# A decoder layer on one core: the first projection without its norm, x on a second queue, and another request order at the MLP's third pair

## The chip, the cores and the metric

The kernel runs on one core of one Trainium2 chip. The metric is the device time of one execution in microseconds, as the median of several runs. The engines are TensorE (PE), VectorE (DVE), ScalarE (ACT), GpSimd (POOL) and SyncE (SP). DMAs are issued by the queues of SP, ACT and POOL.

## What is computed

The reference is one layer of a decoder on 2048 tokens of width 1024, in fp32: a norm, a combined input projection, three causal mixers, an output projection, a gated MLP with a short convolution, and a gated embedding.

```python
h = rmsnorm(x, norm_mix_gain[i])
z = h @ w_in[i]
...
y = jnp.concatenate([y_a, y_b, y_c], axis=-1).astype(dt)
x = x + y @ w_out[i]
x = x + conv_ffn(rmsnorm(x, norm_ffn_gain[i]), ffn_w_up[i], ffn_conv_w[i], ffn_w_down[i])
gate = jax.nn.sigmoid((x @ ple_w_gate[i]).astype(jnp.float32))
x = x + (gate * (p[i] @ ple_w_proj[i]).astype(jnp.float32)).astype(dt)
return rmsnorm(x, final_norm_gain)
```

`rmsnorm(x, g)` is x times 1/sqrt(mean(x^2) + eps) times g. The factor 1/sqrt(...) is one number for each token, so it can also be multiplied into the result of `h @ w_in`.

## The kernel before

**Tiling.** Tokens lie along the free dimension, width along the 128 partitions. There are two halves of 1024 tokens (the loop over `hf`, L465), and each half has two chunks of 512 (`cks`). A tile of 128x1024 (`t4`, from one pool of 40) is one eighth of the width for one half, or two eighths for one chunk.

**fp32 products.** Every operand is split into a high part (ACT copies it, rounded) and a low part (DVE subtracts), by `split` (L256). `mm3` (L264) then makes three matmuls: high x high, high x low and low x high (L265, L266, L267). A tile `h` holds high and low of one eighth of one chunk side by side.

**Weights.** They come as a stream in a fixed order (`wlist`, L210 to L227). `w_get` (L243) hands out a unit and runs the stream ahead by a number of units (`ahead`). A raw unit of 512 KB is loaded on SP's queue into one of three `wr` buffers, then split into `wh` and `wl` (for the projections), or into `wt` tiles (for the MLP, where sums `s` of weight quarters are split too).

**The start (L448 to L461).** SP loads the first chunk of x as four pairs of eighths (`xl`), then constants, the first weight, the vector of gains, the second weight and the second chunk. `Norm.add` squares each eighth on ACT and adds on DVE. `rstd` sums over the partitions by small matmuls into `pm` and takes 1/sqrt in a chain of small DVE steps with one on ACT. `bcast` spreads the result over the partitions by matmuls into `pr`. `h_apply` (L416) multiplies x by the gain and by `pr` (DVE, into `hx`) and splits into `h`.

**The input projection** has 24 units (`IN_UNITS`), each one tile of 128 output rows: two chunks x eight k x three = 48 matmuls into a PSUM pair `pz` (a pool of two). `gemm` (L566) runs the first two units jointly: chunk 0 of both, then chunk 1 of both, so that chunk 1's `h` is wanted later. `evac` (L559) hands a finished PSUM pair to the mixers' functions (`hg_f`, `hg_q`, ..., L557). The mixers' chains (`hg_chain` and two others) run between the projection's steps: `weave` (L593) and `fill` (L584) draw a number of steps of `gemm` between steps of a chain. At the start of the first half `fill` runs eleven steps before and between the second chunk's norm (L728 to L731).

**The MLP** has 22 pairs of gate and up tiles; three matmuls of quarters are saved by sums of weights and of h (the tiles X[0] to X[7]). `up_first` (L879) makes the pairs 0 and 1 together. Its last products go into `pbc`, and after those of pair 0 it does pair 0's convolutions, silu, product and split, and the last steps of `h2`, which makes X[7] and X[4]. `up(j)` (L934) makes the pairs from 2 on; its first product, `pa`, is here called the third pair's start. After every second pair `down_pair` (L965) multiplies two pairs' results with the down weights into `pdn`; ACT copies that to `st`, and POOL's queue adds it to DRAM. `stats_steps` (L1007) loads the next half's x by eighths and squares it for the next norm, one step after each `up(j)`.

**What sets the order.** The instructions are put into each engine's queue by a scheduler, which may put an instruction ahead of others that the program names first; each engine then works its queue in order. Waits between engines follow the data, and the buffers of the pools.

Of the kernel before, what the change touches and what calls it, by code (L numbers as in the profile page):

```python
# [20 lines left out]
CH = 512  # L21
# [27 lines left out]
def trunk(ctx, tc, xT, pT, w_in, w_out, w_up, w_down, w_pp, w_pg, wr_bd, wi_bd, vecs, consts, masks, out):  # L49
# [40 lines left out]
    def cks(c):  # L90
        return slice(c * CH, (c + 1) * CH)
# [187 lines left out]
    def run(g):  # L279
        for _ in g:  # L280
            pass
# [141 lines left out]

    def stats_stream(hf, c):
        n = Norm()
        for k in range(KD):
            s = t2("xs")
            nc.gpsimd.dma_start(s, xT[k, :, hf * TH + c * CH : hf * TH + (c + 1) * CH])
            n.add(s)
        n.rstd()  # L430
        return n
# [16 lines left out]
    x_load(x0[0], 0, 0, nc.sync)  # L448
    nc.sync.dma_start(kt, consts[:, :KBLK])
    w_upto(1)  # L450
    nc.sync.dma_start(vt, vecs)
    w_upto(2)
    x_load(x0[1], 0, 1, nc.sync)
    norms = [Norm(), Norm()]
    for k in range(KD):
        norms[0].add(x0[0][k])
    norms[0].rstd()
    pr = norms[0].bcast()
    for k in range(KD):
        norms[1].add(x0[1][k], nc.gpsimd, True)  # L460
    run(h_apply(h[0], x0[0], "g1", pr))  # L461
# [3 lines left out]
    for hf in range(NH):  # L465
# [93 lines left out]
        def evac(m, ps):  # L559
            for b0, fn in EVAC:  # L560
                if b0 <= m < b0 + (3 if b0 < 18 else 2):
                    fn(m - b0, ps)
# [3 lines left out]
        def gemm():  # L566

            ws, pss = [w_get("in", hf, m) for m in IN_UNITS[:2]], [ps2("pz"), ps2("pz")]
            for c in range(NC):
                for i in range(2):  # L570
                    yield from proj_gen(pss[i][:, cks(c)], ws[i], h[c])
                    if c == NC - 1:
                        evac(IN_UNITS[i], pss[i])
                        done[0] += 1
            for m in IN_UNITS[2:]:
                w, ps = w_get("in", hf, m), ps2("pz")
                for c in range(NC):
                    yield from proj_gen(ps[:, cks(c)], w, h[c])
                evac(m, ps)
                done[0] += 1  # L580
# [146 lines left out]
        if first:  # L727
            fill(6)  # L728
            norms[1].rstd()
            fill(5)  # L730
            run(h_apply(h[1], x0[1], "g1", norms[1].bcast(), (1, 3, 5)))  # L731
            with tc.issue_after(last_split[0].ins), tc.issue_after(last_split[1].ins):
                derived()
            t = t4("blk")[:, :P]
            nc.scalar.dma_start(t, consts[:, KBLK:])
            ACT(blk, t, AF.Copy)
# [141 lines left out]

        def up_first():  # L879
# [33 lines left out]
            for j in pairs:  # L913
                for i in range(2):
                    prod(sums1[j][i], w[j, 2 + i], X[3], False, True)
                    TT(zs[j, i][:, C1], zs[j, i][:, C1], sums1[j][i], op=ADD)
                if j == 0:
                    g_conv(0)
                    u_conv(0)
                    g_silu(0)  # L920
                    gu_mul(0)
                    gu_split(0)
                    run(h2)
                else:
                    g_conv(1)

# [7 lines left out]
        def up(j):  # L934
# [5 lines left out]
            if j % 2 == 0 or j == NJ - 1:  # L940
                g_silu(j - 1)
            prod(B, w_mlp(5, hf, j), X[5], True, False)
            ACT(zu[:, C1], B, AF.Copy)
# [4 lines left out]
            ACT(zg[:, C1], A, AF.Copy)  # L948
            gu_mul(j - 1)
            Cc = ps1(name="pc")  # L950
            prod(Cc, w_mlp(2, hf, j), X[2], True, True)
            TT(zg[:, C0], zg[:, C0], Cc, op=ADD)
            gu_split(j - 1)
            prod(B, w_mlp(3, hf, j), X[3], False, True)
# [66 lines left out]
        for j in range(FIRST, NJ):  # L1021
            up(j)
            next(stats, None)
# [170 lines left out]
```

## Time and profile before

| | |
|---|---|
| time, median of 3 runs | 2505.47 us |
| lowest and highest of them | 2500.73 and 2506.73 us |
| the profiled execution's own time | 2501.25 us |
| its span, first to last instruction | 2499.5 us |
| mean granted clock of TensorE | 0.992 of full speed |

The profile comes from one execution. A timeline row gives the start, the duration, the engine, the line in the kernel, the instruction with its output and inputs, how often it repeats, and in brackets the idle time before it with the instruction that ended it. The matmul records are modelled: a row of 0.39 us means a pipelined matmul whose next one starts earlier than that. A granted clock of 1.00 is 2.4 GHz, of 0.5 is 1.2 GHz.

### The profile page before, as it was taken

The numbers are of one execution on the slowest core, as the hardware profiler recorded it, in microseconds if no ns is written. First come the engines' busy times: TensorE is split into PE (matmuls) and PEld (weight loads), VectorE is DVE, ScalarE is ACT, GpSimd is POOL, SyncE is SP. The second block draws the span as 40 slices with busy tenths as digits, with TensorE's granted clock in tenths as the row PEclk, the third lists the DMA queues.
The fourth block names the chain that finished last, engine by engine and source line by source line (L and its number), as shares of the span: only waits on it lengthen the run. The fifth ranks groups of instructions, "written<-read, shape, count | busy, mean of one in ns | idle before, by whom it ended". The sixth has DMA issues, their size and how long they took to land.

```text
span 2499.5 us, 33974 instructions
## 1 busy us (share of the span) xinstructions
PE 2423.0 (97%) x13660; PEld 1991.4 (80%) x13660; DVE 1578.3 (63%) x2396; ACT 1253.3 (50%) x1696; POOL 192.2 (8%) x240
## 2 busy tenths in 40 slices
PE   5999999889999999999999999998999999999998
PEld 4787788668888888888887787886888888888888
DVE  6566555585555565587565756567666666666856
ACT  5244873355555555545343457734555555555443
POOL 2000001001111111100110000010111111111000
PEclk9999999999999999999999999999999999999999
DMA  3101115435555555533431111251555555555442
GB/s 138 44 28 38 46 54 175 132 95 137 136 135 131 137 136 141 128 137 118 139 105 35 36 35 55 80 189 43 127 132 138 130 127 127 132 134 122 144 144 93
DMA packets 116542, 271.84 MB, mean 109 GB/s; under 512 B 11552, under 2 KB 39840, under 8 KB 116384
## 3 DMA queue, kind: packets, MB, share of 16 engines
q0 software_dynamic: 29056, 104.87, 19.9%
q1 hardware_dynamic: 86320, 163.78, 19.9%
q8 instruction: 107, 1.75, 0.3%
q10 hardware_dynamic: 1008, 1.02, 0.2%
q14 instruction: 51, 0.42, 0.1%
HBM read 177.34 MB, written 92.27 MB: 108 GB/s over the span
## 4 chain that ended last, share of the span: by engine, by line
PE 70%; DVE 4%; ACT 4%; issue 3%; DMA 2%; POOL 0%; SPq 0%; DVEq 0%; ACTq 0%; POOLq 0%
PE pdn L265 6%; PE pdn L267 6%; PE pdn L266 6%; PE pa L265 6%; PE pa L266 6%; PE pa L267 6%; PE pb L267 3%; PE pb L266 3%; PE pb L265 3%; PE pz L265 3%; PE pz L267 2%; PE pz L266 2%; PE pgt L265 2%; PE pgt L267 2%; PE pgt L266 2%
## 5 line engine op out<-in xcount | busy, mean ns | idle before, releaser
L265 PE MATMUL pz<-h,wh 128*128 128x512 f32 x768 | 306.8, 400 | 9.6 <-ACT h L258 9.6
L266 PE MATMUL pz<-h,wh 128*128 128x512 f32 x768 | 301.9, 394 | 2.0 <-DVE h L259 1.7
L267 PE MATMUL pz<-h,wl 128*128 128x512 f32 x768 | 300.7, 392 | 0.0
L265 PE MATMUL pa<-h,wt 128*128 128x512 f32 x672 | 265.1, 395 | 14.3 <-ACT wt L258 14.1
L265 PE MATMUL pdn<-ahi,wt 128*128 128x512 f32 x704 | 274.5, 390 | 1.3 <-ACT st L976 1.3
L267 PE MATMUL pdn<-ahi,wt 128*128 128x512 f32 x704 | 273.9, 389 | 0.0
L266 PE MATMUL pdn<-alo,wt 128*128 128x512 f32 x704 | 273.9, 389 | 0.0
L266 PE MATMUL pa<-h,wt 128*128 128x512 f32 x672 | 264.2, 393 | 0.0
L267 PE MATMUL pa<-h,wt 128*128 128x512 f32 x672 | 263.3, 392 | 0.2 <-DVE wt L259 0.2
L976 ACT ACTIVATE st<-pdn 128x1024 f32<-128x1024 f32 x144 | 147.8, 1027 | 193.6 <-PE pdn L267 182.1
L259 DVE TENSOR_TENSOR wt<-s,wt 128x512 fp32r<-128x512 f32 x160 | 108.4, 688 | 192.1 <-ACT wt L258 192.0
L977 POOL DMA_DIRECT2D xd<-st x144 | 123.2, 855 | 1035.1 <-ACT st L976 1034.4
L265 PEld LDWEIGHTS pz<-h,wh 128*128 128x128 f32 x768 | 145.0, 189 | 41.2 <-ACT h L258 10.7
L266 PEld LDWEIGHTS pz<-h,wh 128*128 128x128 f32 x768 | 145.2, 189 | 34.2 <-DVE h L259 4.6
L267 PEld LDWEIGHTS pz<-h,wl 128*128 128x128 f32 x768 | 145.2, 189 | 30.0
L259 DVE TENSOR_TENSOR wl<-wr,wh 128x1024 fp32r<-128x1024 f32 x120 | 146.2, 1226 | 34.1 <-ACT wh L258 34.0
L265 PEld LDWEIGHTS pa<-h,wt 128*128 128x128 f32 x672 | 127.6, 190 | 42.9 <-ACT wt L258 15.6
L265 PEld LDWEIGHTS pdn<-ahi,wt 128*128 128x128 f32 x704 | 132.1, 188 | 29.7 <-ACT st L976 2.5
L267 PEld LDWEIGHTS pdn<-ahi,wt 128*128 128x128 f32 x704 | 132.1, 188 | 27.7
L266 PEld LDWEIGHTS pdn<-alo,wt 128*128 128x128 f32 x704 | 132.2, 188 | 27.3
L267 PEld LDWEIGHTS pa<-h,wt 128*128 128x128 f32 x672 | 127.5, 190 | 28.4 <-DVE wt L259 1.7
L266 PEld LDWEIGHTS pa<-h,wt 128*128 128x128 f32 x672 | 127.7, 190 | 26.4
(273 smaller groups left out, 5058.6 us busy)
## 6 DMA issues: line engine op xcount, KB each, us to landing
xd<-st POOLq DMA_DIRECT2D x144, 512.0 KB, 6.3
wr<-in_w_up SPq DMA_DIRECT2D x176, 256.0 KB, 4.2
wr<-in_w_in SPq DMA_DIRECT2D x48, 512.0 KB, 3.5
q<-in_w_down SPq DMA_DIRECT2D x88, 256.0 KB, 3.4
wr<-in_w_pg SPq DMA_DIRECT2D x40, 512.0 KB, 4.4
wr<-in_w_out SPq DMA_DIRECT2D x32, 512.0 KB, 3.6
q<-in_w_up SPq DMA_DIRECT2D x40, 256.0 KB, 3.1
xr<-in_xT POOLq DMA_DIRECT2D x32, 256.0 KB, 4.0
```

The lines of the kernel that those rows point to most:

```text
L259: last_split[:] = i, (eng or nc.vector).tensor_tensor(lo, src, hi.bitcast(F32), op=SUB)
L265: MM(ps, wk[0], rk[0], start=start, stop=False, **kw)
L266: MM(ps, wk[0], rk[1], start=False, stop=False, **kw)
L267: MM(ps, wk[1], rk[0], start=False, stop=stop, **kw)
L976: ACT(st, ps, AF.Copy)
L977: nc.gpsimd.dma_start(xd[m], st, accum_op=ADD)
```

## The change

At the **start**, the program asks SP's queue for the gains, weights, the second chunk of x and the constants, and ScalarE's queue for the first chunk of x. In the first half h is x times the gain alone, split at once (`h_raw`): ACT makes the high part with the gain as its scale, DVE the low part. So the projection does not wait for the norm. `evac` multiplies each finished PSUM pair by `rn`, the spread 1/rms, with two DVE multiplications into a tile `zr`, from which the mixers' functions then read. The first three units run jointly in the first half (the third in two single PSUM tiles); in the second half, where the norm is known early, none do. Both norms are made after the first two steps of `gemm`.

At the **third pair** of the MLP, the third pair's first weight is asked for right after pair 0's sums, and pair 0's silu, product and split and the last two steps of `h2` go to a list, `early`, from which `later()` takes one at each of five places in `up(2)`. The `stats` steps start after j = 3.

```diff
--- before.py
+++ after.py
@@ -421,6 +421,13 @@
             dst[k] = split_chunk(s, "h", nc.gpsimd if k in pool else None)
             yield
 
+    def h_raw(dst, xs, gain, ks):
+
+        for k in ks:
+            t = dst[k] = t4("h", F32R)
+            ACT(t[:, :CH], xs[k], AF.Copy, scale=vec(gain, k))
+            STT(t[:, CH:], xs[k], vec(gain, k), t[:, :CH].bitcast(F32), op0=MUL, op1=SUB)
+
     def stats_stream(hf, c):
         n = Norm()
         for k in range(KD):
@@ -445,20 +452,18 @@
             eng.dma_start(t.rearrange("p (k t) -> p k t", k=2), xT[k : k + 2, :, t0 : t0 + CH].rearrange("k p t -> p k t"))
             xs += [t[:, :CH], t[:, CH:]]
 
-    x_load(x0[0], 0, 0, nc.sync)
-    nc.sync.dma_start(kt, consts[:, :KBLK])
+
+
+    nc.sync.dma_start(vt, vecs)
     w_upto(1)
-    nc.sync.dma_start(vt, vecs)
+    x_load(x0[0], 0, 0, nc.scalar)
     w_upto(2)
     x_load(x0[1], 0, 1, nc.sync)
+    nc.sync.dma_start(kt, consts[:, :KBLK])
     norms = [Norm(), Norm()]
-    for k in range(KD):
-        norms[0].add(x0[0][k])
-    norms[0].rstd()
-    pr = norms[0].bcast()
-    for k in range(KD):
-        norms[1].add(x0[1][k], nc.gpsimd, True)
-    run(h_apply(h[0], x0[0], "g1", pr))
+    h_raw(h[0], x0[0], "g1", range(KD))
+    w_upto(3)
+    h_raw(h[1], x0[1], "g1", range(KD))
     nc.vector.memset(hcar, 0.0)
     nc.vector.memset(scar, 0.0)
 
@@ -557,6 +562,11 @@
         EVAC = [(9, hg_f), (6, hg_q), (12, hg_v), (15, hg_g), (0, rg_u), (3, rg_g), (20, sc_c), (22, sc_v), (18, sc_b)]
 
         def evac(m, ps):
+            if first:
+                t = t4("zr")
+                for c in range(NC):
+                    TT(t[:, cks(c)], ps[c], rn[:, cks(c)], op=MUL)
+                ps = t
             for b0, fn in EVAC:
                 if b0 <= m < b0 + (3 if b0 < 18 else 2):
                     fn(m - b0, ps)
@@ -564,19 +574,25 @@
         done = [0]
 
         def gemm():
-
-            ws, pss = [w_get("in", hf, m) for m in IN_UNITS[:2]], [ps2("pz"), ps2("pz")]
-            for c in range(NC):
-                for i in range(2):
-                    yield from proj_gen(pss[i][:, cks(c)], ws[i], h[c])
-                    if c == NC - 1:
-                        evac(IN_UNITS[i], pss[i])
-                        done[0] += 1
-            for m in IN_UNITS[2:]:
+            n = 0
+            if first:
+
+                n = 3
+                ws = [w_get("in", hf, m, ahead=1) for m in IN_UNITS[:n]]
+                pss = [ps2("pz"), ps2("pz")]
+                pss = [[t[:, cks(c)] for c in range(NC)] for t in pss] + [[ps1(name="pz"), ps1(name="pz")]]
+                for c in range(NC):
+                    for i in range(n):
+                        yield from proj_gen(pss[i][c], ws[i], h[c])
+                        if c == NC - 1 and i:
+                            for u in ([0, 1] if i == 1 else [i]):
+                                evac(IN_UNITS[u], pss[u])
+                                done[0] += 1
+            for m in IN_UNITS[n:]:
                 w, ps = w_get("in", hf, m), ps2("pz")
                 for c in range(NC):
                     yield from proj_gen(ps[:, cks(c)], w, h[c])
-                evac(m, ps)
+                evac(m, [ps[:, cks(c)] for c in range(NC)] if first else ps)
                 done[0] += 1
 
         G = gemm()
@@ -725,10 +741,16 @@
                 ys[c][k] = split_chunk(y[k][:, cks(c)], "ys")
 
         if first:
-            fill(6)
-            norms[1].rstd()
-            fill(5)
-            run(h_apply(h[1], x0[1], "g1", norms[1].bcast(), (1, 3, 5)))
+            rn = t4("rn")
+            fill(2)
+            for c in range(NC):
+                for k in range(KD):
+                    norms[c].add(x0[c][k], None, True)
+            for c, q in enumerate((23, 7)):
+                fill(q)
+                norms[c].rstd()
+                fill(3)
+                ACT(rn[:, cks(c)], norms[c].bcast(), AF.Copy)
             with tc.issue_after(last_split[0].ins), tc.issue_after(last_split[1].ins):
                 derived()
             t = t4("blk")[:, :P]
@@ -876,6 +898,12 @@
             split(hi, lo, zs[j, "g"])
             acts[j] = (hi, lo)
 
+        early = []
+
+        def later():
+            if early:
+                early.pop(0)()
+
         def up_first():
 
             pairs = range(FIRST)
@@ -915,14 +943,13 @@
                     prod(sums1[j][i], w[j, 2 + i], X[3], False, True)
                     TT(zs[j, i][:, C1], zs[j, i][:, C1], sums1[j][i], op=ADD)
                 if j == 0:
+                    w_upto(wat[5, hf, FIRST] + 1)
                     g_conv(0)
                     u_conv(0)
-                    g_silu(0)
-                    gu_mul(0)
-                    gu_split(0)
-                    run(h2)
                 else:
                     g_conv(1)
+
+            early.extend([lambda: g_silu(0), lambda: next(h2, None), lambda: gu_mul(0), lambda: gu_split(0), lambda: next(h2, None)])
 
         banks = {}
 
@@ -939,18 +966,23 @@
             ACT(zg[:, C0], A, AF.Copy)
             if j % 2 == 0 or j == NJ - 1:
                 g_silu(j - 1)
+            later()
             prod(B, w_mlp(5, hf, j), X[5], True, False)
+            later()
             ACT(zu[:, C1], B, AF.Copy)
             if j > FIRST:
                 last_prod(j - 1)
             u_conv(j - 1)
             prod(A, w_mlp(6, hf, j), X[6], False, False)
             ACT(zg[:, C1], A, AF.Copy)
+            later()
             gu_mul(j - 1)
             Cc = ps1(name="pc")
             prod(Cc, w_mlp(2, hf, j), X[2], True, True)
             TT(zg[:, C0], zg[:, C0], Cc, op=ADD)
+            later()
             gu_split(j - 1)
+            later()
             prod(B, w_mlp(3, hf, j), X[3], False, True)
             TT(zg[:, C1], zg[:, C1], B, op=ADD)
             prod(A, w_mlp(7, hf, j), X[7], False, False)
@@ -1020,7 +1052,8 @@
         stats = iter(()) if last else stats_steps()
         for j in range(FIRST, NJ):
             up(j)
-            next(stats, None)
+            if j > 3:
+                next(stats, None)
             if j % 2 == 0 and j < NJ - 2:
                 down_pair(j // 2 - 1, lambda: g_silu(j))
         run(stats)
```

Three places show how the order of the queues moves.

ACT's queue at the start (wr: a raw weight, wh: its high part, xl: x, sq: a square, hx: x scaled by norm and gain, h: the split operand). Before:

```order
L436 ACTIVATE warm<-epsc 128x1
L306 ACTIVATE sq_119<-xl_89 128x512
L306 ACTIVATE sq_139<-xl_95 128x512
L258 ACTIVATE wh_100<-wr_98 128x1024
L320 ACTIVATE v_147<-v_147 128x4
L258 ACTIVATE wh_107<-wr_105 128x1024
L258 ACTIVATE h_185<-hx_183 128x512
```

and now:

```order
L443 ACTIVATE warm<-epsc 128x1
L258 ACTIVATE wh_92<-wr_90 128x1024
L452 DMA xl_96<-in_xT 128x2x512
L452 DMA xl_102<-in_xT 128x2x512
L258 ACTIVATE wh_106<-wr_104 128x1024
L428 ACTIVATE h_119<-xl_96,vt 128x512
L428 ACTIVATE h_140<-xl_102,vt 128x512
L258 ACTIVATE wh_145<-wr_143 128x1024
L306 ACTIVATE sq_199<-xl_96 128x512
```

The x loads are now issued by ACT's queue behind the first weight's split, the splits of x follow with no norm ahead of them, and the squares come after all splits of both chunks.

DVE's queue where the fifth unit of the projection needs its weight (zr: an evicted unit, pl: PE's products within chunks, pd: sums over heads, wl: a weight's low part), now:

```order
L568 TENSOR_TENSOR zr_505<-pz_191,rn_182 128x512
L568 TENSOR_TENSOR zr_505<-pz_192,rn_182 128x512
L650 COPY_PREDICATED acc_178<-mk_181,pl_615 128x128x2
L626 SCALAR_TENSOR_TENSOR dv_464<-v_508,pd_587 128x512
L626 SCALAR_TENSOR_TENSOR dv_464<-v_508,pd_591 128x512
L259 TENSOR_TENSOR wl_513<-wr_510,wh_512 128x1024
L259 TENSOR_TENSOR wl_519<-wr_516,wh_518 128x1024
```

and PE's queue at the same place (wl_513 is the low part that DVE makes there), now:

```order
L267 MATMUL pz_522<-h_170,wl_186 128x512
L354 MATMUL pd_595<-lp_476,blk 128x512
L355 MATMUL pd_595<-lp_476,blk 128x512
L643 MATMUL pl_615<-Q_463,K_449 64x32 x16
L643 MATMUL pl_616<-Q_463,K_449 64x32 x15
L265 MATMUL pz_582<-h_119,wh_512 128x512
L266 MATMUL pz_582<-h_119,wh_512 128x512
L643 MATMUL pl_616<-Q_463,K_449 64x32
L267 MATMUL pz_582<-h_119,wl_513 128x512
```

PE's third matmul of the fifth unit needs wl_513, which DVE makes behind a COPY_PREDICATED that needs pl_615; before the change another whole unit of the projection stood between PE's fourth unit and these products.

DVE's queue at the third pair, first half (pbc: the last sums of the pairs 0 and 1, gu: the convolved gate and up, alo: a result's low part, wt: split weights, s: sums of weights, h: X tiles). Before:

```order
L916 TENSOR_TENSOR zg_3898<-zg_3898,pbc_4108 128x512
L410 SCALAR_TENSOR_TENSOR gu_4200<-zg_3898,vt,gu_4200 128x1023
L410 SCALAR_TENSOR_TENSOR gu_4200<-zg_3898,vt,gu_4200 128x1022
L308 TENSOR_TENSOR sq_4416<-sq_4416,sq_6061 128x512
L872 TENSOR_TENSOR gu_4200<-gu_4200,gu_4205 128x1024
L259 TENSOR_TENSOR alo_4213<-gu_4200,ahi_4212 128x1024
L259 TENSOR_TENSOR h_4217<-h_487_3653,h_4217 128x512
L259 TENSOR_TENSOR h_4229<-h_488_3654,h_4229 128x512
L259 TENSOR_TENSOR wt_4270<-wr_4267,wt_4270 128x512
L259 TENSOR_TENSOR wt_4279<-s_4276,wt_4279 128x512
L172 TENSOR_TENSOR s_4276<-wr_4273,s_4276 128x512
```

and now:

```order
L259 TENSOR_TENSOR wt_4247<-wr_4244,wt_4247 128x512
L167 TENSOR_TENSOR s_4253<-s_4253,wr_4244 128x512
L259 TENSOR_TENSOR wt_4256<-s_4253,wt_4256 128x512
L259 TENSOR_TENSOR wt_4304<-s_4253,wt_4304 128x512
L944 TENSOR_TENSOR zg_3942<-zg_3942,pbc_4152 128x512
L410 SCALAR_TENSOR_TENSOR gu_4259<-zg_3942,vt,gu_4259 128x1023
L410 SCALAR_TENSOR_TENSOR gu_4264<-zu_3943,vt,gu_4264 128x1023
L894 TENSOR_TENSOR gu_4259<-gu_4259,gu_4264 128x1024
L259 TENSOR_TENSOR h_4358<-h_498_3698,h_4358 128x512
L259 TENSOR_TENSOR wt_4368<-s_4253,wt_4368 128x512
L259 TENSOR_TENSOR alo_4408<-gu_4259,ahi_4407 128x1024
L259 TENSOR_TENSOR alo_4412<-gu_4295,ahi_4411 128x1024
```

The third pair's first weights (wt_4247 to wt_4304) now stand ahead of the sums and the conv steps, where they stood behind the conv steps, the product, alo and the four last h splits; the square sums among the conv steps (sq) are gone from here.

## Rows read from the trace of the kernel before

**Rows 1.** The page's part 1: busy time, share and instructions of each engine.

```profile
PE 2423.0 (97%) x13660; PEld 1991.4 (80%) x13660; DVE 1578.3 (63%) x2396; ACT 1253.3 (50%) x1696; POOL 192.2 (8%) x240
```

**Rows 2.** The page's part 4: the chain that ended last, by engine.

```profile
PE 70%; DVE 4%; ACT 4%; issue 3%; DMA 2%; POOL 0%; SPq 0%; DVEq 0%; ACTq 0%; POOLq 0%
```

**Rows 3.** Timeline of PE at the start (start, duration, instruction, [idle before and releaser]).

```profile
26.36 0.79 PE L265 MATMUL pz<-h,wh 128*128 128x512 f32 x1 [8.40 <-ACT h L258]
...
34.52 1.22 PE L316 MATMUL pm<-kt,sq 128*128 128x1 f32 x8
...
37.45 0.63 PE L265 MATMUL pz<-h,wh 128*128 128x512 f32 x1
...
37.87 0.63 PE L266 MATMUL pz<-h,wh 128*128 128x512 f32 x1
...
80.62 0.39 PE L266 MATMUL pz<-h,wh 128*128 128x512 f32 x1
...
80.85 0.39 PE L267 MATMUL pz<-h,wl 128*128 128x512 f32 x1
```

**Rows 4.** Timeline at the start: SP's queue, ACT and DVE.

```profile
0.74 1.97 SPq L445 DMA_DIRECT2D xl<-in_xT  x4
...
5.01 1.15 ACT L306 ACTIVATE sq<-xl 128x512 f32<-128x512 f32 x2 [2.30 <-DMA xl<-in_xT]
...
9.15 1.15 ACT L306 ACTIVATE sq<-xl 128x512 f32<-128x512 f32 x2 [0.23 <-DMA xl<-in_xT]
...
18.00 2.72 DVE L420 SCALAR_TENSOR_TENSOR hx<-xl,vt,pr 128x512 f32<-128x512 f32 x4 [1.02 <-PE pr L332]
...
25.70 2.17 ACT L258 ACTIVATE h<-hx 128x512 fp32r<-128x512 f32 x4
```

**Rows 5.** Timeline of PE at the third pair, first half.

```profile
519.34 0.39 PE L267 MATMUL pbc<-h,wt 128*128 128x512 f32 x1
527.72 0.80 PE L265 MATMUL pa<-h,wt 128*128 128x512 f32 x1 [7.99 <-ACT wt L258]
```

**Rows 6.** Timeline of DVE and of ACT at the third pair, first half.

```profile
522.76 1.22 DVE L872 TENSOR_TENSOR gu<-gu,gu 128x1024 f32<-128x1024 f32 x1
...
524.98 2.17 ACT L258 ACTIVATE h<-h 128x512 fp32r<-128x512 f32 x4
...
527.06 0.61 ACT L258 ACTIVATE wt<-wr 128x512 fp32r<-128x512 f32 x1
```

**Rows 7.** Busy time by stretches: each engine, granted clock, DMA share, GB/s.

```profile
520.00:530.00 10.00, 2.26 (x5) 1.35 (x6) 10.00 (x13) 6.62 (x11) 0.00 (x0) 0.66 0.09 26
530.00:540.00 10.00, 10.00 (x38) 8.07 (x37) 8.76 (x15) 5.94 (x10) 0.00 (x0) 0.83 0.50 159
```

**Rows 8.** Timeline of PE at the third pair, second half.

```profile
1749.07 0.80 PE L265 MATMUL pa<-h,wt 128*128 128x512 f32 x1 [5.60 <-ACT wt L258]
...
1751.38 0.63 PE L266 MATMUL pc<-h,wt 128*128 128x512 f32 x1
```

**Rows 9.** Groups of DVE between 60 and 440 us (count, busy, mean ns, idle before).

```profile
L259 DVE TENSOR_TENSOR wl<-wr,wh 128x1024 fp32r<-128x1024 f32 x36 | 43.8, 1221 | 11.6 <-ACT wh L258 11.6
...
L634 DVE COPY_PREDICATED acc<-mk,pl 128x256 f32<-128x256 int32 x30 | 14.1, 496 | 12.8 <-PE pl L627 12.7
...
L762 DVE TENSOR_TENSOR x<-xr,po 128x512 f32<-128x512 f32 x12 | 8.2, 687 | 23.7 <-PE po L267 22.4 <-DMA xr<-in_xT 1.3
```

**Rows 10.** Busy time of the stretch of 20 us with most of DVE, first half's mixers.

```profile
200.00:220.00 20.00, 18.84 (x318) 15.04 (x317) 16.82 (x27) 3.31 (x4) 0.00 (x0) 1.00 0.04 8
```

**Rows 11.** Timeline at the start of the second half: PE's first projection, POOL's last split.

```profile
1267.61 0.48 PE L265 MATMUL pz<-h,wh 128*128 128x512 f32 x1
...
1278.09 1.29 POOL L259 TENSOR_TENSOR h<-hx,h 128x512 fp32r<-128x512 f32 x1 [0.90 <-ACT h L258]
```

**Rows 12.** Group of DVE from 500 to 551 us: the sums of squares.

```profile
L308 DVE TENSOR_TENSOR sq<-sq,sq 128x512 f32<-128x512 f32 x10 | 6.9, 685 | 0.1
```

**Rows 13.** Timeline of PE in the first down product.

```profile
559.42 0.50 PE L265 MATMUL pdn<-ahi,wt 128*128 128x512 f32 x1 [1.32 <-ACT st L976]
```

## The prediction

> **What bounds the kernel now.** First the page's busy line: PE is busy 2423.0 of 2499.5 us, DVE 1578.3 [rows 1]. The chain that ended last is PE for 70%, with DVE and ACT 4% each [rows 2]. So a change pays only where PE waits or runs at the lower clock, and the timeline of PE alone shows where. Its 128x512 matmuls start 0.227 us apart (80.62 and 80.85, taken over several rows); at the lower of its two levels (1.2 against 2.4 GHz) 0.425 apart (37.45 and 37.87) [rows 3].
>
> Two places matter. At the **start** the first projection matmul begins at 26.36 us [rows 3], because of a chain: x lands and is squared (5.01 to 10.3), the squares are summed and the norm spread by small matmuls, and only then is x scaled (18.00) and split (25.70) [rows 4]. PE then works at half clock at first (0.79 us for one at 26.36) and again at 37.87; the projection's 192nd matmul starts at 80.85, though 192 x 0.227 are only 43.6 us [rows 3]. At the **MLP's third pair** PE stands for 8.15 us: the matmul after 519.34 starts at 527.72, released by ACT's split of a weight [rows 5]. ACT comes to that split at 527.06 because its queue holds four h splits first (524.98), which stand behind the split of pair 0's product, and that waits for DVE's mul (522.76) behind the conv steps [rows 6]. DVE is busy 10.00 of the 10 us there, and the granted clock is 0.66 [rows 7]. The second half has the same wait, 5.60 us before 1749.07, with matmuls of 0.63 behind it [rows 8].
>
> **The start.** Removed are, in the first half, the scaling by the norm and the split of the scaled copy. Added are 16 ACT splits with a scale (0.54 us each: 2.17 for four) and 16 DVE subtractions with a gain (0.68: 2.72 for four) [rows 4], which wait for x alone. ACT's queue now holds the first weight's split ahead of its x loads (the order above). The first of SP's loads released ACT 4.3 us after its issue at 0.74; the pairs behind it came 1.4 apart ((9.15 - 5.01)/3) [rows 4]. So the first weight, second on SP's queue, lands near 5.0, the x loads issue from 5.1 on (SP took 0.5 us for each [rows 4]), and the first pair can land by 9.4.
>
> What x shares the way with is new: two weights on SP's queue and the second chunk. Bounds: 1.4 us between pairs, as if alone; 2.8, shared evenly. I take the even share, because SP issues a weight and chunk 1 while ScalarE's loads are under way, and 0.5 for the first: pairs at 9.9, 12.6, 15.3 and 18.0. The Trainium skill, DMA: Bandwidth & Descriptors, section "Issuing engines are not separate DMA queues", says that loads issued from SP, ScalarE and GpSimd run on the same 16 engines and interleave, so that by it the second queue brings no bandwidth. By it the last pair comes at 18.0; were the queues apart it would come at 13.6. No run here has yet shown both queues loading at once.
>
> So the first matmul comes at 10.5 (9.9 and a split of 0.6) against 26.36. Unit 0's 24 matmuls on chunk 0 keep pace with x and end near 21. The 48 of units 1 and 2 need 10.9 us at full clock; some 3 us of them at half speed add 1.4: chunk 0 ends near 33. Chunk 1 is 72 x 0.227 = 16.3, with both norms' small matmuls between (1.22 for one norm's sums [rows 3], the spreading taken as long: at most 4.9, of which I take 3, since they run beside others): 52.5. The fourth unit ends 10.9 later, at 63.4, against 81.1: a lead of 17.7.
>
> Then something is late next. In DVE's new order the subtraction that makes unit 4's low weights stands behind two evictions, a COPY_PREDICATED that waits for PE's score products, and two dv steps; PE wants it at unit 4's first k, and before the change another whole unit stood between. One row of 0.5 us, two of 0.69 and one of 1.22 [rows 9] make 3.1, the products ahead of them 0.5: **3.6 us lost**. Start: 17.7 - 3.6 = **14 us gained**, bounds 8 (x at 4 us between pairs, chunk 0 all at half clock) and 18 (no wait).
>
> **Evictions.** 24 units x 2 = 48 DVE multiplications out of PSUM, 0.687 us each by a row that reads PSUM already [rows 9]: 33 us of DVE. What hides them: of the 19 stretches of 20 us from 60 to 440 the one in which DVE is fullest has 16.82 [rows 10]. 33 us over 380 are 1.7 for each, so even that one stays under 20. If DVE falls behind for a moment, PE waits where it waits already: that stretch has 18.84 of PE. Between 0 and 6 us, I take **2 lost**.
>
> **Joint units.** The second half has none now: 24 matmuls (5.4 us) stand between the first use of chunk 0's h and of chunk 1's, not 48. Its projection starts at 1267.61; chunk 1's last h is split on POOL from 1278.09 to 1279.38 [rows 11]. Chunk 1 would start at 1273.1 and come to its last k 21 matmuls or 4.8 us later, at 1277.9. Between 0 and 1.5, I take **0.5 lost**.
>
> **Third pair, first half.** Its weights are now split before g_conv(0), and pair 0's silu, mul and split and the rest of h go in between its products. The new order of DVE (above) has the weights ahead of the conv steps, so PE's 8.15 us go, and with them the half clock behind them: 0.17 of the 10 us from 530 on and half of the 2.3 before them [rows 7], 2.8, **10.9 together**. Late next is pair 1's low half, which the first down product needs. From 512 us, the first of the four last sums, DVE has until then eight conv steps (1.2 each, like the mul [rows 6]), some fifteen steps of 0.6 (sums, h, weights) and four of 1.15 (mul, splits of the products), with small ones 24.8: 536.8, while PE comes there at 519.6 + 72 x 0.227 = 536.0. The square sums (ten of them in 500 to 551 [rows 12]) no longer stand between, 6 us. Bounds 3 and 11, I take **9.5 gained**.
>
> **Third pair, second half.** 5.60 and the half clock behind it (0.2 for each of seven matmuls, 1.3): 6.9, and up to 1 of the small wait before. Bounds 4 and 8, I take **7 gained**. The squares of the next half's norm start later; in the profile one of them, waiting for its load, held the eviction of a down product and PE 1.32 us [rows 13]. They now come with j over 3. Between 1.5 gained and 1.5 lost, **1 gained**.
>
> **Sum.** 14 + 9.5 + 7 + 1 - 2 - 0.5 = 29. The profiled run took 2501.25 us, its span 2499.5; less 29 is 2472.2. The median of the runs lies 4.2 above the profiled run, so 2476.
>
> **Rivals.**
> *Start paced by x.* If three streams share the way evenly, pairs come 4.1 apart, the last at 22; PE works chunk 0 in short pieces at half clock (72 x 0.2 = 14 us dearer, of which the pace covers a part). The lead is some 5 us instead of 14: 2485. For it: the half clock at 26.36 and 37.87 [rows 3]. Against: with four k already split it did rise in between.
> *The wait moves to the down product.* If DVE is the bound at the third pair (10.00 of 10 us [rows 7]), PE's wait goes from 519 to the first down product, and only the square sums and a part of the clock are gained, about 4 + 3 instead of 16.5: 2486. Both rivals at once give 2495.
> *Evictions bind (slower).* Two PSUM pairs serve the units, so PE must wait once DVE is over one unit (10.9 us) behind. Every unit then pays its two multiplications, 1.37, and 1.3 for the clock after a stop, as after 1749: 21 units x 2.7 = 57 us, 2533. It decides when DVE reaches 20 of 20; 16.82 + 1.7 speaks against.
> *The first matmuls come early and nothing follows.* The recurrence behind the first unit needs rn, which comes only after both chunks are squared. If PE waits there, and again for the chains behind it, the start is given back; with the second rival the time is 2498 to 2500: no change.
>
> **Chances.** My forecast 0.62, start paced 0.12, wait moved 0.14, nothing follows 0.07, evictions 0.05. About 0.3% (7.5 us) is what a measurement of this kernel can tell from no change: faster 0.88, same 0.07, slower 0.05. The range goes from all gains at their upper bounds (18 + 11 + 8 + 1.5 and no loss: 2467, less 4 for the spread of the runs) up to both of the first rivals nearly at once: 2463 to 2494.
>
> **What would show it.** Right: the first projection matmul near 10.5 us, the 192nd near 63, then a wait of some 3.6 us for a weight's low half; no wait over 2 us between the sums and the third pair, clock 1.00 there; the first down product 16 to 17 us after the sums. Wrong: x pairs over 3 us apart, PE waiting for the zr tile, PE waiting for alo at the first down product, or stretches of 20 us with DVE at 20 in the first half's mixers.

## The result, and the profile after

The change takes 2474.24 us (median of 4 runs, 2473.66 to 2478.15) against 2503.34 of the kernel before (4 runs, 2500.73 to 2506.73). The ratio is 0.9893 with a 95% interval of 0.9878 to 0.9907: 1.1% faster. The profiled execution took 2474.39 us, its span is 2472.6 us, and so 26.9 us shorter than the span of before; the medians differ by 29.1. The forecast was 2476.

The page's part 1 and the engines' line of part 4, after:

```profile
PE 2419.8 (98%) x13660; PEld 1990.1 (80%) x13660; DVE 1597.6 (65%) x2438; ACT 1255.5 (51%) x1700; POOL 177.3 (7%) x230
...
PE 67%; issue 18%; ACT 6%; DVE 5%; DMA 3%; POOL 2%; ACTq 0%; POOLq 0%; DVEq 0%; SPq 0%
```

PE does the same 13660 matmuls in about the same busy time [rows 1]; what became shorter is the time in which it stands. DVE has 19 us more: 33 us of evictions came, and scaling and splits went. The chain that ended last is "issue" for 18% where it was 3% [rows 2]; that is time in which the profile shows no wait, and nothing below is read from it.

Where the time came from is read best from one table. For the same matmul, counted from the start, it gives its start time in the profile of before, and how much earlier it starts in the change and in four of the experiments below (worked out from the timelines of PE). That number is called the lead below; where it falls, the kernel loses time against the one before.

| matmul | before, us | change | only_start | only_mlp | stats_behind | best |
|---|---|---|---|---|---|---|
| first of the projection | 26.36 | 14.5 | 13.6 | -0.1 | 14.9 | 14.9 |
| 192nd of it | 80.85 | 14.7 | 14.0 | 0.4 | 15.4 | 19.1 |
| 240th | 95.69 | 12.0 | 8.5 | 0.4 | 12.7 | 19.1 |
| 768th | 265.30 | 12.2 | 8.7 | 0.4 | 12.9 | 19.3 |
| last of the first half | 365.97 | 14.8 | 11.2 | -0.6 | 15.4 | 21.9 |
| first of the MLP | 453.37 | 8.1 | 3.5 | -2.5 | 8.8 | 13.3 |
| first of down-projection, first half | 547.06 | 25.3 | 5.4 | 12.9 | 26.4 | 32.2 |
| first gate matmul (pgt) | 1155.21 | 18.4 | 4.8 | 5.2 | 28.3 | 33.7 |
| second half's first projection | 1267.60 | 18.4 | 4.8 | 5.2 | 28.3 | 33.7 |
| first of down-projection, second half | 1767.33 | 27.9 | 5.4 | 15.6 | 38.4 | 44.0 |
| last of all | 2491.92 | 26.9 | 5.7 | 15.7 | 37.2 | 43.5 |

Each column is one execution. `again`, below, is the change in another one, the longest of its four; it has 9.1 at the 240th matmul, 4.3 at the MLP, 21.1 at the first down product, 11.4 at the gate and 20.2 at the end. So a few us between two columns can be of the execution and not of the edit. The profile of only_start, too, is of the longest of its runs (2495.60 us, their median is 2492.14). What is read from a lead below is read from how it moves over one step, and from several profiles where there are some.

**The start.** ACT's timeline of the change, from the first weight on:

```profile
5.11 1.06 ACT L258 ACTIVATE wh<-wr 128x1024 fp32r<-128x1024 f32 x1 [2.44 <-DMA wr<-in_w_in]
5.12 2.15 ACTq L452 DMA_DIRECT2D xl<-in_xT  x4
...
11.07 1.33 ACT L428 ACTIVATE h<-xl,vt 128x512 fp32r<-128x512 f32 x2 [2.54 <-DMA xl<-in_xT]
12.64 1.33 ACT L428 ACTIVATE h<-xl,vt 128x512 fp32r<-128x512 f32 x2 [0.23 <-DMA xl<-in_xT]
15.80 1.34 ACT L428 ACTIVATE h<-xl,vt 128x512 fp32r<-128x512 f32 x2 [1.83 <-DMA xl<-in_xT]
18.51 1.34 ACT L428 ACTIVATE h<-xl,vt 128x512 fp32r<-128x512 f32 x2 [1.37 <-DMA xl<-in_xT]
```

The first weight came at 5.11, the x loads were issued from 5.12 on, beside the split, and the pairs came at 11.07 to 18.51, 2.5 us apart on average: the even share. PE's timeline, at the four places where the start decides:

```profile
11.85 0.79 PE L265 MATMUL pz<-h,wh 128*128 128x512 f32 x1 [11.85 <-ACT h L428]
...
34.41 1.05 PE L316 MATMUL pm<-kt,sq 128*128 128x1 f32 x8 [1.33 <-DVE sq L308]
35.32 0.66 PE L265 MATMUL pz<-h,wh 128*128 128x512 f32 x1
...
69.82 1.11 PE L643 MATMUL pl<-Q,K 64*64 64x32 f32 x30 [0.90 <-DVE acc L650]
...
72.06 0.50 PE L267 MATMUL pz<-h,wl 128*128 128x512 f32 x1 [0.24 <-DVE wl L259]
```

PE starts at 11.85 where it started at 26.36 [rows 3]. It waits 1.33 us for the norm's sums, runs at half clock behind that (the granted clock is 0.64 from 36 to 40 us), and around 70 us stops in pieces for the first recurrence and the fifth unit's low weights.

**The third pair.** Busy time by stretches there, after (PE, PEld, DVE, ACT, POOL, clock, DMA share, GB/s):

```profile
510.00:520.00 10.00, 10.00 (x46) 8.28 (x45) 10.00 (x14) 5.60 (x8) 0.00 (x0) 1.00 0.26 80
520.00:530.00 10.00, 10.00 (x46) 8.25 (x45) 9.32 (x16) 7.24 (x10) 1.74 (x2) 1.00 0.46 113
530.00:540.00 10.00, 8.63 (x37) 6.47 (x35) 3.35 (x5) 3.96 (x6) 1.71 (x2) 1.00 1.00 215
540.00:550.00 10.00, 8.93 (x33) 7.31 (x34) 2.28 (x4) 6.07 (x9) 2.89 (x4) 0.83 1.01 200
```

Against [rows 7], PE has no wait before the third pair and full clock, with DVE as full as before. PE is short of work a little later, in the first down-projection (530 to 550). PE's and ACT's timelines show why:

```profile
541.07 0.79 PE L265 MATMUL pdn<-ahi,wt 128*128 128x512 f32 x1 [2.41 <-ACT st L1008]
541.67 0.63 PE L266 MATMUL pdn<-alo,wt 128*128 128x512 f32 x1
...
584.50 0.50 PE L265 MATMUL pa<-h,wt 128*128 128x512 f32 x1 [0.60 <-ACT zg L977]
589.55 0.50 PE L266 MATMUL pdn<-alo,wt 128*128 128x512 f32 x1 [0.76 <-DVE alo L259]
```

```profile
534.01 0.63 ACT L306 ACTIVATE sq<-xs 128x512 f32<-128x512 f32 x1 [2.63 <-DMA xs<-in_xT]
...
539.48 0.63 ACT L306 ACTIVATE sq<-xs 128x512 f32<-128x512 f32 x1 [3.41 <-DMA xs<-in_xT]
540.02 1.01 ACT L1008 ACTIVATE st<-pdn 128x1024 f32<-128x1024 f32 x1
...
583.33 0.63 ACT L306 ACTIVATE sq<-xs 128x512 f32<-128x512 f32 x1 [2.34 <-DMA xs<-in_xT]
```

A square that waits 3.41 us for its load stands in ACT's queue ahead of the eviction `st`, and PE waits for that eviction. In the profile of before there was one such wait of PE [rows 13]; 14 of the 16 squares had run there before the first down product. In the change 11 of them run from 529 to 584, and the lead shrinks from 25.3 to 18.4 us. In the nine other profiles that have the MLP's edits, or most of them, and do not move the squares away, it shrinks by 5 to 10 us over the same stretch.

### The profile page after: what moved, and what is told of

It reads as the page before. It is cut to its first block, busy times and chain, and to the rows that moved or that the text cites. A ratio compares the mean times of both kernels' runs of the same rounds, so it can differ in the third digit from the quotient of the medians.

```text
span 2472.6 us, 34027 instructions
## 1 busy us (share of the span) xinstructions
PE 2419.8 (98%) x13660; PEld 1990.1 (80%) x13660; DVE 1597.6 (65%) x2438; ACT 1255.5 (51%) x1700; POOL 177.3 (7%) x230
## 4 chain that ended last, share of the span: by engine, by line
PE 67%; issue 18%; ACT 6%; DVE 5%; DMA 3%; POOL 2%; ACTq 0%; POOLq 0%; DVEq 0%; SPq 0%
PE pz L265 5%; PE pz L267 5%; PE pz L266 5%; PE pdn L265 5%; PE pdn L266 5%; PE pdn L267 5%; PE pa L265 4%; PE pa L267 4%; PE pa L266 4%; PE pgt L265 2%; PE pgt L266 2%; PE pgt L267 2%; PE pb L267 2%; PE pb L266 2%; PE pb L265 2%
```

## The experiments

Twelve kernels ran, four to a chip, each beside runs of the kernel before on that chip. Ratios are against those.

**only_start** leaves the MLP as before:

```diff
-                    w_upto(wat[5, hf, FIRST] + 1)
                     g_conv(0)
                     u_conv(0)
+                    g_silu(0)
+                    gu_mul(0)
+                    gu_split(0)
+                    run(h2)
...
-            early.extend([lambda: g_silu(0), lambda: next(h2, None), lambda: gu_mul(0), lambda: gu_split(0), lambda: next(h2, None)])
...
-            if j > 3:
-                next(stats, None)
+            next(stats, None)
```

> Only the start's edits (x on ScalarE's queue, no norm before the projection, rn at the evictions, joint units), with the MLP and its square sums as before. Theory that the two parts add: the lead at the end of the first half's mixers is 12 us as in the profile of the change, nothing else moves, 2503.3 - 12.5 = 2491. Rival, evictions cost more than the profile shows because the changed MLP hides it: 2496 to 2500.

Measured: 2492.14 us (10 runs) against 2499.90, ratio 0.9967 (0.9957 to 0.9977), a gain of 8 us, between the 12.5 of the theory and the 3 to 7 of the rival. In its profile the lead of 14.0 us falls to 8.5 between the 192nd and the 240th matmul, and to 3.5 at the MLP. So the start's edits by themselves are worth less than the 12 us that stand in the mixers of the change.

**only_mlp** is the kernel before with the MLP's edits alone (the same lines, the other way).

> Only the MLP's edits (third pair's weight first, pair 0's steps spread, square sums after j = 3) on the start of before. Theory that the two parts add: 7.8 us in the first half and 8.8 in the second, 2503.3 - 16.5 = 2487. Rival, the wait of the first half is gone only because PE arrives at another time: 2490 to 2495.

Measured: 2485.49 against 2499.90, ratio 0.9950 (0.9935 to 0.9964), a gain of 12.5 by the ratio. By the table it gains 13 us up to the first down-projection, gives back 7.7 and gains about 10 in the second half. The two parts come to 20.8 us together and the change to 26.8 by its ratio. The missing 6 us are about as much as the three intervals together leave open (2.5 us on only_start, 3.6 on each of the others), so whether the parts add is not shown.

**stats_early** undoes `if j > 3`.

> The change, but with the square sums from the third pair on as before. Theory: the late sums only move a cost; 6 us of the lead that the first down product has are given back between 521 and 610 us where squares wait for their loads in ACT's queue, and with the early sums DVE has them before the first down product: 2473 to 2476, the first down product some 5 us later. Rival 1, the late sums were needed to free DVE: 2479 or more. Rival 2, they are a loss: 2470 or less.

Measured: 2472.58, ratio 0.9895 (0.9880 to 0.9910): no difference to the change. The first down product did not come later, and the lead again falls from 28.0 there to 19.5 at the gate. Its last 11 squares run from 527 to 582 us, at the same place as in the change. So the condition in the loop decides nothing: the scheduler sets loads and squares into the down-projection with it and without it.

**x_on_sp** replaces `nc.scalar` by `nc.sync` for the first chunk.

> The change, but the first chunk of x is loaded by SP's queue, behind three weights and ahead of chunk 1. Theory that both queues share one way: the pairs of x come 1.4 us apart and are there by 12 to 13 us instead of 18.5, chunk 0 ends 2 to 4 us earlier, and as PE then waits longer for the norm's sums only 1 to 3 us are left: 2471 to 2473. Rival, the second queue brings bandwidth: first matmul later than 11.85, 2476 or more.

Measured: 2470.51, ratio 0.9893 (0.9879 to 0.9908), that of the change. ACT's timeline:

```profile
5.64 1.06 ACT L258 ACTIVATE wh<-wr 128x1024 fp32r<-128x1024 f32 x1 [2.96 <-DMA wr<-in_w_in]
...
10.99 5.34 ACT L428 ACTIVATE h<-xl,vt 128x512 fp32r<-128x512 f32 x8 [2.12 <-DMA xl<-in_xT]
```

Behind three weights on one queue the first pair comes at 10.99, as early as on the second queue (11.07), and the other pairs behind it without a wait. The 144th matmul then has a lead of 19.6 instead of 14.7 us, and by the MLP 10.7 instead of 8.1. The second queue is not what brings the start forward; for the whole time no difference can be told. The DMA engines are as full with two queues loading as with one, and move as much (from 11 to 18 us, the change first, then x_on_sp):

```profile
11.00:18.00 7.00, 6.15 (x14) 4.49 (x15) 4.24 (x6) 4.01 (x6) 0.00 (x0) 1.00 1.05 396
...
11.00:18.00 7.00, 6.24 (x18) 4.67 (x19) 6.11 (x9) 6.96 (x11) 0.00 (x0) 1.00 1.05 392
```

**again** is the change once more, as a measure for the three that follow.

> The change itself, once more, beside the runs of the kernel before on the same chip as the three that follow: ratio 0.987 to 0.991; PE's wait for the fifth unit's low weights 2 to 3 us of gaps and, where the clock drops behind it, up to 3 us more.

Measured: 2474.57 (2472.15 to 2481.01), ratio 0.9894 (0.9879 to 0.9910). Its profile is of the longest of its runs. Between 60 and 80 us it shows what differs (the change first, then again):

```profile
60.00:80.00 20.00, 18.87 (x180) 15.12 (x178) 16.48 (x23) 6.75 (x8) 0.00 (x0) 1.00 0.22 67
...
60.00:80.00 20.00, 19.10 (x123) 15.04 (x123) 16.55 (x23) 6.75 (x8) 0.00 (x0) 0.83 0.21 67
```

The same stop at the fifth unit costs 2.7 us of the lead in the change and 5.5 here (14.7 before it, 9.1 behind it). PE waits 0.90 us for DVE's `acc` in both; what differs is the granted clock, 1.00 there and 0.83 here. only_start, too, loses 5.5 there.

**stats_behind** loads each part of the next half's x one step ahead, and queues its square and sum behind the step's last weight split:

```diff
+                if i < NC * KD:
+                    s, o = t2("xs"), T0 + TH + i // KD * CH
+                    nc.sync.dma_start(s, xT[i % KD, :, o : o + CH])
+                if held is not None:
+                    with tc.issue_after(last_split[0].ins), tc.issue_after(last_split[1].ins):
+                        n.add(held)
...
+                held = s
```

> The change, but each load of the next half's x is issued one step ahead of its square, and the square and its sum are queued behind the last weight split of that step on ACT and DVE. Theory: the lead is given back between 521 and 610 us because squares that wait for their loads stand in ACT's and DVE's queues ahead of evictions; so PE's waits at 541, 584 and 589 us go, 4 to 6 us faster than the change run beside it. Rival, the loads themselves hold POOL's accumulating DMAs: no more than 1 us.

Measured: 2464.97 (2463.58 to 2468.62), ratio 0.9854 (0.9840 to 0.9869), 9.6 us faster than `again` beside it: more than expected. The first square in ACT's timeline, and the stretches of the first down-projection:

```profile
619.15 0.62 ACT L306 ACTIVATE sq<-xs 128x512 f32<-128x512 f32 x1
```

```profile
520.00:540.00 20.00, 20.00 (x90) 16.54 (x89) 9.84 (x15) 11.61 (x16) 5.12 (x6) 1.00 0.80 166
540.00:560.00 20.00, 20.00 (x90) 16.58 (x89) 12.00 (x16) 11.41 (x17) 1.72 (x2) 1.00 0.62 151
```

The squares run from 619 us on and no longer wait for their loads, PE is busy all of the 40 us, and the lead grows to 28.3 us at the gate instead of falling to 18.4. The edit moves the loads too, out of the first down-projection; so the wait in the queue and the loads' share of the DMA engines are not told apart by this run alone (a row of `best`, below, speaks for the queue).

**w5_early** asks for the fifth unit's weights before chunk 1 of the joint units:

```diff
                 for c in range(NC):
+                    if c == 1:
+                        w_upto(5)
                     for i in range(n):
```

> The change, but the fifth unit's weights are asked for before chunk 1 of the three joint units, so that DVE makes their low half ahead of the norm and the first recurrence. Theory: PE's wait there goes, 2.7 us faster than the change beside it, up to 5 where the clock dropped. Rival, PE then waits at the next place for the same chain (the sixth unit or the second score product): under 1 us.

Measured: 2473.92, ratio 0.9889 (0.9875 to 0.9904), 0.7 us less than `again`. DVE now makes the low weights at 38 us, and the lead stays at 15.4 from the 192nd to the 240th matmul; of the 3.4 us that this is ahead of the change 2.9 are left at the MLP's first matmul and 1.1 at the last of its first products. So the expected wait was there and went, but the time is not the 2.7 us of the theory shorter: a later place takes most of it back.

**zr_twice** runs each of the 48 multiplications a second time.

```diff
                 for c in range(NC):
                     TT(t[:, cks(c)], ps[c], rn[:, cks(c)], op=MUL)
+                    TT(t[:, cks(c)], ps[c], rn[:, cks(c)], op=MUL)
```

> The change, but each of the 48 multiplications out of PSUM runs twice (33 us more of DVE in the first half's mixers; the output is the same). Theory that DVE has the room: 2 to 6 us slower than the change beside it, all of it at the start and at the passage to the output projection, none at the units between. Rival, evictions bind: 20 us or more slower.

Measured: 2482.55 (2480.10 to 2485.17), ratio 0.9923 (0.9907 to 0.9940), 8.0 us slower than `again`: more than the theory's 6, far less than the rival's 20. Its stretches at the start and in the middle:

```profile
60.00:80.00 20.00, 17.01 (x111) 13.62 (x110) 17.08 (x25) 5.59 (x8) 0.00 (x0) 0.74 0.17 53
200.00:220.00 20.00, 20.00 (x281) 16.03 (x275) 18.56 (x35) 7.84 (x9) 0.00 (x0) 1.00 0.09 29
```

With DVE at 18.56 of 20 PE still has no gap in the middle, and the lead is 7.5 us at the 240th matmul and 8.3 at the 768th. It is lost at the fifth unit, where the clock falls to 0.74: 8.4 us of the lead between the 192nd and the 240th matmul, against 2.7 in the change and 5.5 in again. At the passage to the output projection it loses 9.0, against 7.1 and 8.1.

**best** takes `x_on_sp`, `w5_early` and `stats_behind` together.

> The change with three edits: x's first chunk by SP's queue, the fifth unit's weights asked for before chunk 1, each square queued a step behind its load. If they add: 9.6 us (squares) and 1 to 5 (the two at the start, of which the passage to the MLP takes a part) faster than the change: 2460 to 2464 beside a kernel before of 2502, ratio 0.983 to 0.985. Rival, the start's two edits bring nothing once the passage from mixers to MLP is reached: the same as the squares alone, 0.9854.

Measured: 2456.33 (2454.67 to 2458.63) against 2498.09, ratio 0.9830 (0.9811 to 0.9849). It is faster than the kernel before, and than the change, whose interval ends at 0.9878. Against `stats_behind` (0.9854) the intervals overlap, so what the start's two edits add is open, though its lead at the MLP is 13.3 against 8.8. A stretch of 20 us in its first down-projection:

```profile
520.00:540.00 20.00, 20.00 (x90) 16.58 (x89) 5.62 (x10) 11.68 (x15) 6.32 (x8) 1.00 1.03 206
```

The DMA engines are as full as in the change at 530 to 550 (1.03 against 1.00), without loads of xs between, and PE does not wait: full DMA engines alone did not stop it here.

**joint2** runs the second half's first two units jointly again.

> The change, but the second half's first two units run jointly as before. Theory that 24 matmuls are cover enough (the profile shows PE losing 0.01 us there): no difference, ratio 0.988 to 0.991. Rival, the joint units hid the last h split: 1 us faster.

Measured: 2477.93, ratio 0.9919 (0.9896 to 0.9941), whose interval overlaps that of the change (to 0.9907). At the place itself neither kernel has a gap: the lead before and behind the first 48 matmuls of the second half is 18.37 and 18.38 in the change, 15.62 and 15.61 here. What this run is behind lies elsewhere, and is not more than the intervals leave open.

**weight_only** keeps the early request and puts pair 0's steps back, **list_only** keeps the list and drops the request:

```diff
 weight_only
                     w_upto(wat[5, hf, FIRST] + 1)
                     g_conv(0)
                     u_conv(0)
+                    g_silu(0)
+                    gu_mul(0)
+                    gu_split(0)
+                    run(h2)
...
 list_only
-                    w_upto(wat[5, hf, FIRST] + 1)
```

> The change, but of the MLP's edits only the early request of the third pair's first weight and the late squares: pair 0's silu, product and split and the last h steps stand where they stood. Theory that PE's 8 us were the order of ACT's queue at the weight's split: only two of the third pair's weights come ahead, so PE starts the third pair at once but waits 3 to 5 us at the next weights, in both halves: 6 to 9 us slower than the change. Rival, the early request alone does it: the same as the change.

> The change, but without the early request: pair 0's steps still go in between the third pair's products, the weight is asked for as before. Theory: with pair 0's product and split gone from ahead of it, the weight's split comes early all the same: within 2 us of the change. Rival, both are needed: 6 us or more slower.

Measured on one chip: weight_only 2482.91, ratio 0.9936 (0.9916 to 0.9956); list_only 2475.26, ratio 0.9905 (0.9882 to 0.9928). PE's timeline of weight_only:

```profile
514.71 0.50 PE L265 MATMUL pa<-h,wt 128*128 128x512 f32 x1 [2.26 <-ACT wt L258]
...
516.23 0.79 PE L265 MATMUL pb<-h,wt 128*128 128x512 f32 x1 [0.18 <-ACT zu L974]
```

With the request alone PE starts the third pair at once and then waits at its later weights, as expected. From 514 us to the first down product the lead grows by 12.5 us in the change and in list_only, by 7.9 in weight_only, and not in only_start; in the second half by 8.9, 8.9 and 5.4. So the list alone brings the whole gain. The request alone brings some three fifths of it, and beside the list nothing that can be seen.

## Why the prediction was right, and where its steps failed

The median was right within 2 us, and the change was faster as forecast. The steps were less good than their sum, and that their errors cancel to 2 us is in part luck:

- **Start, 14 us forecast, 12.0 measured** (the lead at the 240th matmul; 9.1 in again). The landing of x was right (9.9, 12.6, 15.3 and 18.0 forecast; 11.07, 12.64, 15.80 and 18.51 measured), and with it the rival by which x paces the start fell. The Trainium skill, DMA: Bandwidth & Descriptors, section "Issuing engines are not separate DMA queues", says that loads issued from several engines run on the same 16 DMA engines and interleave. The traces agree: 396 GB/s with two queues, 392 with one (x_on_sp). Chunk 0 ended near 33 as forecast, but "52.5" for the end of chunk 1 was 55.2, and the 192nd matmul came at 66.1 and not near 63: the step left out that PE waits 1.33 us for the norm's sums and then runs some 3.5 us at half clock. The wait at the fifth unit was named at 3.6 us and measured 2.7 in this profile; w5_early takes it away. The larger part of PE's standing there is for DVE's `acc` (0.90 us), which stands ahead of the low weights on DVE (0.24). The rival by which nothing follows from the early start fell as well: 8.1 us of the lead are left at the MLP.
- **Evictions, 2 us lost forecast, about none.** The lead is 12.0 at the 240th matmul and 12.7 at 514 us. Over the same stretch the other ten profiles with these evictions lie between 2.8 lost and 1.6 gained, and zr_twice, with twice the evictions, loses 0.1. zr_twice also shows the reserve of the middle, so the rival by which evictions bind is refuted at this load. Between, the lead moves. At the passage from the mixers to the output projection it falls by 7.1: PE waits for `sqp` of the head norm, which in ACT's queue stands behind ten splits of `ys`, and later for a `ys` (below, PE and then ACT). Then 4.9 come back by 478, where before had longer waits of its own (1.65 us at 445.30, 1.83 at 458.99, 2.22 at 468.80; 0.80, 1.60 and 1.08 in the change). What set the order at the passage is not shown. only_mlp loses nothing there, the profiles with the start's edits 6.4 to 8.3, and zr_twice 9.0: it comes with the start's edits and depends little on the number of evictions. The prediction had no such term.

```profile
353.90 1.02 PE L354 MATMUL pmh<-sqp,blk 128*128 128x512 f32 x2 [2.30 <-ACT sqp L258]
365.64 0.49 PE L265 MATMUL po<-ys,wh 128*128 128x512 f32 x1 [2.06 <-ACT ys L258]
```

```profile
345.94 2.18 ACT L258 ACTIVATE ys<-dv 128x512 fp32r<-128x512 f32 x4
348.03 3.22 ACT L258 ACTIVATE ys<-u 128x512 fp32r<-128x512 f32 x6
...
353.23 1.14 ACT L258 ACTIVATE sqp<-sqh 128x512 fp32r<-128x512 f32 x2
```

- **Joint units, 0.5 lost forecast, none measured** (a lead of 18.37 before the first 48 matmuls of the second half and 18.38 behind them).
- **Third pair, first half: 9.5 gained forecast, 12.5 measured** at the first down product (a lead of 12.7 at 514, 25.3 there): 8.15 of wait, 2.8 of half clock and 1.2 of a small wait that [rows 5] do not show (the row of before below). The gain is the same 12.5 in all eleven profiles with the list, from different starts. DVE came in time: PE did not wait for alo there. The rival by which the wait moves to the down product is refuted. list_only shows that the steps of pair 0 stood in the way, as the prediction read it from ACT's queue: with them gone the weight need not be asked for earlier. weight_only shows that an earlier request gets round a part of them.

```profile
516.72 0.50 PE L265 MATMUL pbc<-h,wt 128*128 128x512 f32 x1 [1.17 <-DVE zg L916]
```

- **The squares: this step failed.** The prediction took "1 gained" for their later start, between 1.5 gained and 1.5 lost. The mechanism was named (a square that waits for its load holds the eviction of a down product), its size and sign were not seen: 6.9 us of the lead were given back from 521 us to the gate. The forecast counted the square sums out of DVE's way before the down product and did not ask where the 11 squares would stand instead. stats_early shows that the condition in the loop is not the cause. stats_behind shows that the 16 squares and their loads are: with them moved the lead grows by 1.8 over the same stretch. That it is the squares' place in ACT's queue and not the loads is read from the rows and from the stretch of best, and no run parts the two.
- **Third pair, second half: 7 forecast, 8.9 measured** (a lead of 19.0 at 1720, 27.9 at the first down product). There is no next half's norm there, and the lead holds.

By these steps the forecast's 9.5 + 1 stands against 12.5 - 6.9 = 5.6, its 14 - 2 against 12.7 and its 7 against 8.9: 4.9 forecast too much and 2.6 too little. With 0.5 for the joint units, 0.6 gained in the second half's mixers and 0.9 lost at the end, the 29 forecast become the 26.9 by which the span is shorter. This is the account of one profile; by the times of only_start and only_mlp the two parts come to 20.8. So the forecast's mechanism held at the start and at both third pairs; it failed at the squares, and its number was saved by gains elsewhere that were larger than forecast.

## What to carry to other kernels

When a stall goes, the next thing to look for is what the scheduler had put into it: work that filled the wait (here squares that wait for their own loads) moves into a stage without room, and an instruction that waits for a DMA holds what is queued behind it on its engine (a square that waited 3.41 us held an eviction, and PE 2.41 us). Issue such a load a step ahead and queue its consumer behind work that ends later: here that gave 9.6 us. The added evictions cost nothing that shows in the middle of the mixers, while the kernel with the new start lost 2.7 us at the fifth unit and 7.1 at the passage to the output projection: price each passage, not the mean. And take a second profile of the same kernel before a few us between two profiles are read as the work of an edit.

## What was not expected of the hardware

The same stop of PE near 70 us cost 2.7 us in one profile of the same kernel and 5.5 in another, since the granted clock over the 20 us around it was 1.00 in the one and 0.83 in the other; the prediction priced it without the clock. And the DMA engines at a mean busy share of 1.03 over 20 us, with POOL's accumulating transfers on them, did not make PE wait (best, 520 to 540 us).
